# Joint 512-column mLSTM projections, an earlier last key, and a reordered opening in a two-layer mixer kernel on one core

## The chip, the cores and the metric

The kernel runs on one core of one Trainium2 chip. The metric is the device time of that core in microseconds. TensorE (PE) multiplies, VectorE (DVE) and ScalarE (ACT) work on vectors, GpSimd (POOL) does a few helpers, SyncE (SP) issues the DMAs. TensorE takes weights of 128 x 128 and streams 128 to 512 columns past them; its results land in PSUM, which has eight banks of 512 fp32 columns per partition here.

## The reference, cut to what matters

1024 latent tokens and 256 context tokens of width 1024 pass through two layers. Each layer has one input projection, eight bidirectional mLSTM heads and eight neighbourhood attention heads, one output projection and a squared-ReLU MLP.

```python
for l in range(DEPTH):                       # 2
    need_ctx = l < DEPTH - 1
    mod = silu_c @ w_ada[l] + b_ada[l]       # six shifts, scales and gates
    h  = rmsnorm(x,  norm1_g[l]) * (1.0 + sc1)  + sh1
    hc = rmsnorm(xc, norm1_g[l]) * (1.0 + sc1c) + sh1c
    y, yc = token_mixers(h @ w_in[l], hc @ w_in[l], ...)
    x = x + g1 * (y @ w_out[l])
    x = x + g2 * sq_relu_mlp(h2, w_mlp1[l], w_mlp2[l])
# mLSTM, per head, 64-token chunks, both directions:
s   = einsum('bhtd,bhsd->bhts', q, k) * w_intra
num = w_prev * (q @ C) + s @ v;   h = num / max(|qn|, exp(-m))
C   = w_c * C + (w_s * k)^T v
y   = head_layernorm(h_fwd + h_bwd) * sigmoid(o)
```

`w_in` has columns q, k, v, o of the mLSTM, q, k, v of the attention and the gates. The context rows of layer 1 are only read as keys and values, so its queries and gates o are not computed.

## The kernel before, in words

Products are made in fp32 from three passes: each operand is split into a rounded high part and a rest, and `mm3` (L85 to L87) adds high x high, high x rest and rest x high in PSUM. A weight chunk of 128 x 1024 is loaded to `wraw` (2 buffers), cast by ScalarE to `whi` (L79) and subtracted by the vector engine to `wlo` (L80); there are 4 pairs of split buffers. PSUM is cut into two banks of tag "mm" for projections and six of tag "q" for the rest.

Tokens are taken in five tiles of 256 (tile 0 is the context). In the opening (0 to some 57 us) x, the modulation weights and the first weights are loaded, x is squared, scaled and normed, and the first projections run on half of the depth. L1410 and L1411 sum the squares, L1416 scales x, L149 multiplies by the modulation weights, L171 copies their row of sums, L174 turns it, L184 makes the factor A, L1426 and L868 apply it and split x.

Then `mlstm_kv` projects keys, values and gates of the first head pair (288 columns), `gates` makes the decay tables (L329, L349), and `na_values` projects the first half of the attention's values, copied to `wraw` by L619 and stored. The pair's keys are rotated (`rope`, L399 to L403), turned by TensorE (L421, copied by L422), weighted (`vw`, L468), multiplied to chunk states (L470) and linked forwards (L478) and backwards (L459).

`mlstm_out` takes four head pairs by five tiles (four tiles in layer 1). For each it projects q and o of this pair, 256 columns, two token blocks side by side in one "mm" bank. Beside it runs a second generator, `along`: it projects k and v of the next pair, also 256 columns, or for the last pair the second half of the attention's values. Each projection is 48 matmuls of 256 columns. A tile then goes on: exponential of o (L529), rope, transposes of q (L550) and their copy (L552), scores and state product (L561, L562), weights `wt` (L545), P (L571), P·V (L573), normalizing (L576 to L599), transposes of the result (L603) and their store. After the stage the attention starts with its own key and query projections at 512 columns.

The order within each engine is fixed when the program is built; the generators' yields decide which pieces meet, and small steps of the next layer's modulation (`fill`, L149) are strung between.

## Time and profile before

| | |
|---|---|
| median of 3 runs | 2970.12 us (2970.05 to 2971.06) |
| profiled execution | 2972.53 us |
| its span, first to last instruction | 2970.7 us |
| mean granted TensorE clock | 0.995 |
| TensorE, vector engine, ScalarE busy | 98%, 71%, 42% |
| opening | 0 to 57 us |
| first pair, gates, values | 57 to 129.4 and 1640 to 1717.7 us |
| mLSTM stage, layers 0 and 1 | 129.4 to 472.6 and 1717.7 to 2018.5 us |

The other time is neighbourhood attention, output projection and MLP of both layers. Matmul records overlap: a matmul's busy time contains its drain, while the next has begun. So the step from one start to the next tells how fast TensorE gets on, and the idle column what it waited for.

### The profile page before, as it was taken

What the parts mean: (1) busy time and instruction counts of PE and PEld (TensorE: products, weight loads), DVE (VectorE), ACT (ScalarE), POOL (GpSimd) and SP (SyncE); (2) the same over time, 40 slices, a digit from 0 to 9 for tenths busy, and PEclk for the clock granted to TensorE, in tenths of its full rate; (3) what the DMA queues carried; (4) which work ended last, traced back from release to release, by engine and by line L of the source; (5) the groups of instructions that cost most, each with busy time, mean ns of one, the idle gap of its engine ahead of it and who ended that gap; (6) DMA issues with size and microseconds to landing.
All of it is one profiled execution on the core that took longest, in us unless ns stands there. A gap on an engine that the chain in (4) does not pass through costs nothing. (4 is left out here: it accounts for less than half of the span.)

```text
span 2970.7 us, 49781 instructions
## 1 busy us (share of the span) xinstructions
PE 2905.2 (98%) x18900; PEld 2515.7 (85%) x18900; DVE 2105.7 (71%) x4805; ACT 1256.3 (42%) x2350; POOL 71.8 (2%) x117
## 2 busy tenths in 40 slices
PE   7999999999999999999999999999999999999998
PEld 4899998888888888888889989998878788888888
DVE  6666786777686655587676667776775887768765
ACT  5322233555463333344454322234554633334453
POOL 0000000001000000000000000000010000000000
PEclk9999999999999999999999999999999999999999
DMA  6444213235545444696765254213346364469673
GB/s 234 159 129 141 67 53 103 79 118 172 176 140 182 143 143 147 232 329 223 260 205 182 75 163 145 93 39 118 97 144 208 114 197 151 156 224 318 217 238 112
DMA packets 295841, 477.21 MB, mean 161 GB/s; under 512 B 20625, under 2 KB 149649, under 8 KB 295601
## 3 DMA queue, kind: packets, MB, share of 16 engines
q1 hardware_dynamic: 295600, 474.04, 48.2%
q8 instruction: 148, 2.42, 0.3%
q14 instruction: 93, 0.75, 0.1%
HBM read 378.37 MB, written 95.58 MB: 160 GB/s over the span
## 5 line engine op out<-in xcount | busy, mean ns | idle before, releaser
L85 PE MATMUL q<-ah,whi 128*128 128x512 f32 (+1 forms) x1512 | 563.6, 373 | 1.1 <-ACT whi L867 0.7
L86 PE MATMUL q<-al,whi 128*128 128x512 f32 (+1 forms) x1512 | 563.0, 372 | 0.0
L87 PE MATMUL q<-ah,wlo 128*128 128x512 f32 (+1 forms) x1512 | 560.9, 371 | 1.1 <-DVE wlo L868 1.1
L85 PE MATMUL mm<-whi,ah 128*128 128x256 f32 (+1 forms) x1440 | 418.3, 290 | 0.2 <-ACT kva L442 0.2
L86 PE MATMUL mm<-wlo,ah 128*128 128x256 f32 (+1 forms) x1440 | 412.7, 287 | 0.0
L87 PE MATMUL mm<-whi,al 128*128 128x256 f32 (+1 forms) x1440 | 412.2, 286 | 0.0
L85 PE MATMUL mm<-ah,whi 128*128 128x512 f32 (+1 forms) x1080 | 372.7, 345 | 0.6 <-ACT ah L826 0.6
L86 PE MATMUL mm<-al,whi 128*128 128x512 f32 (+1 forms) x1080 | 372.3, 345 | 0.0
L87 PE MATMUL mm<-ah,wlo 128*128 128x512 f32 (+1 forms) x1080 | 371.9, 344 | 0.0
L85 PEld LDWEIGHTS q<-ah,whi 128*128 128x128 f32 x1512 | 284.9, 188 | 54.9 <-issue 4.0
L87 PEld LDWEIGHTS q<-ah,wlo 128*128 128x128 f32 x1512 | 285.0, 188 | 51.9 <-DVE wlo L868 1.9
L86 PEld LDWEIGHTS q<-al,whi 128*128 128x128 f32 x1512 | 285.1, 189 | 50.4 <-issue 2.1
L85 PEld LDWEIGHTS mm<-whi,ah 128*128 128x128 f32 x1440 | 277.1, 192 | 8.7 <-issue 4.0
L86 PEld LDWEIGHTS mm<-wlo,ah 128*128 128x128 f32 x1440 | 277.1, 192 | 1.9 <-issue 1.7
L87 PEld LDWEIGHTS mm<-whi,al 128*128 128x128 f32 x1440 | 277.0, 192 | 0.7 <-issue 0.7
L85 PEld LDWEIGHTS mm<-ah,whi 128*128 128x128 f32 x1080 | 204.6, 189 | 26.5 <-ACT ah L826 1.3
L87 PEld LDWEIGHTS mm<-ah,wlo 128*128 128x128 f32 x1080 | 204.8, 190 | 24.8
L86 PEld LDWEIGHTS mm<-al,whi 128*128 128x128 f32 x1080 | 204.6, 189 | 24.6
L867 ACT CAST ah<-raw 128x512 fp32r<-128x512 f32 (+1 forms) x264 | 145.0, 566 | 118.2 <-PE q L87 59.6
L868 DVE TENSOR_TENSOR al<-raw,ah 128x512 fp32r<-128x512 f32 (+1 forms) x264 | 158.4, 620 | 31.0 <-ACT ah L867 30.9
L80 DVE TENSOR_TENSOR wlo<-wraw,whi 128x1024 fp32r<-128x1024 f32 (+2 forms) x90 | 109.3, 1216 | 97.3 <-ACT whi L79 96.2
L868 DVE TENSOR_TENSOR wlo<-raw,whi 128x1024 fp32r<-128x1024 f32 x84 | 102.7, 1223 | 103.6 <-ACT whi L867 103.3
(285 smaller groups left out, 5209.4 us busy)
## 6 DMA issues: line engine op xcount, KB each, us to landing
raw<-w SPq DMA_DIRECT2D x168, 512.0 KB
raw<-hid SPq DMA_DIRECT2D x104, 512.0 KB
wada<-w_ada SPq DMA_DIRECT2D x96, 512.0 KB
wraw<-w SPq DMA_DIRECT2D x80, 512.0 KB
hid<-hb SPq DMA_DIRECT2D x128, 256.0 KB
hid<-ht SPq DMA_DIRECT2D x96, 256.0 KB
gb<-gscr SPq DMA_DIRECT2D x36, 512.0 KB
wraw<-w_out SPq DMA_DIRECT2D x32, 512.0 KB
```

Of the source, the lines that this page charges most:

```text
L80: nc.vector.tensor_sub(lo[:, :n], raw[:, :n], fview(hi[:, :n]))
L85: mm(out, lh, rh, start=start, stop=False, skip_group_check=True)
L86: mm(out, lh, rl, start=False, stop=False, skip_group_check=True)
L87: mm(out, ll, rh, start=False, stop=stop, skip_group_check=True)
L867: ins = self.nc.scalar.copy(hi, src)
L868: self.nc.vector.tensor_sub(lo, src, fview(hi))
```

## The change

1. The weights are laid out anew: `w_j` has for each pair [k and v of the next pair | q and o of this pair], for the last pair [second half of the values | q and o]. `project_j` multiplies them in one go: per token block 24 matmuls of 512 columns into a whole "mm" bank, two banks per tile. Four split chunks serve a pair instead of two and two.
2. `mlstm_tile` gets the projected columns and yields once more, between scores and P·V. The keys' turn, the states and the back links (`kv_turn`, `kv_state`, `kv_back`) are called by the step instead of by a generator beside it. Rope and the copies of o, k and v work on 128 columns of each bank instead of 256 of one.
3. The first pair's last two keys are turned before the values; the values are staged in `kva` buffers instead of `wraw`.
4. The attention's first two key projections (`qk_project`, 256 and 512 columns) are issued in the mLSTM stage's last step.
5. In the opening the squares of the third group, the scalings, the W splits and the norms are ordered anew, with eight buffers of squares instead of four.

```diff
+    def project_j(self, W, i, hi, lo, cols):
+        for u in range(2):
+            acc = self.bank("mm")
+            for k in range(KT):
+                wh, wl = W[k // 2]
+                ws = slice((k % 2) * 512, (k % 2) * 512 + cols)
+                self.mm3(acc[:, :cols], self.toktile(hi[k], 2 * i + u), ...
...
     def mlstm_kv(self, l, hi, lo, W, accs):
...
+            if i > 1:
+                self.kv_turn(0, i - 2)
+            yield
+        self.kv_turn(0, NT // 2 - 2)
+        self.kv_turn(0, NT // 2 - 1)
+        yield
...
     def mlstm_out(self, l, hi, lo, need_ctx, W):
+            if n and i == 0:
+                W = self.joint_weights(l, pr)
+            mine = need_ctx or i > 0
+            accs = self.project_j(W, i, hi, lo, 512 if mine else 256)
+            if pr < 3:
+                self.kv_take(pr + 1, i, accs)
+            else:
+                self.value_store(l, 1, i, [a[:, 0:256].unsqueeze(1) for a in accs])
+            t = self.mlstm_tile(l, pr, i, [a[:, 256:512].unsqueeze(1) for a in accs]) if mine else iter(())
...
+            if n == len(seq) - 1:
+                Wq.extend(self.qk_weights(l, 0, which) for which in (1, 0))
+                keys.append(self.qk_project(Wq[0], 0, hi, lo))
+                next(t, None)
+                run_all(before)
+                keys.append(self.qk_project(Wq[0], 1, hi, lo))
+                run_all(t)
+                return Wq, keys
+            if i == n2 and pr < 3:
+                self.kv_turn(pr + 1, i)
+                self.kv_state(pr + 1, i)
+                self.kv_back(pr + 1)
+            later = ahead(n + 1)
+            next(t, None)
+            next(later, None)
+            run_all(before)
+            if i < n2 and pr < 3:
+                self.kv_turn(pr + 1, i)
+                self.kv_state(pr + 1, i)
             t, before = later, t
...
     def mlstm_tile(self, l, pr, i, acc):
             S.append(sb)
+        yield
         for u in range(2):
...
     def opening(self, xp, ap0, xsrc, hi, lo):
-        q = [squares(0), squares(1)]
-        r = [self.rstd(*z) for z in q]
-        scale(0, r[0])
-        q = squares(2)
-        scale(1, r[1])
-        scale(2, self.rstd(*q))
-        W = [self.split_raw(t, n) for t, (_, n) in zip(raws, chunks)]
-        steps(first, 2)
+        run_all(squares(0, q[0]))
+        run_all(squares(1, q[1]))
+        r0 = self.rstd(*q[0])
+        rest = squares(2, q[2])
+        steps(rest, 2)
+        r1 = self.rstd(*q[1])
+        scale(0, r0)
...
+        W = [self.split_raw(raws[z], chunks[z][1]) for z in range(2)]
+        r2 = self.rstd(*q[2])
+        scale(1, r1)
+        scale(2, r2, range(6))
```

On TensorE, in the mLSTM stage of layer 0, before: a projection of q and o has ended eleven rows earlier, eight modulation matmuls and the scores of the tile before (L561, L562) follow, and from the last score matmul on stands this (ah, al, whi, wlo are the split parts; L573 P·V, L550 and L603 the transposes of q and of the result):

```order
L562 MATMUL q<-cst,qT 128x130
L573 MATMUL q<-kva,P 128x65 x4
L85 MATMUL mm<-whi,ah_87 128x256
L86 MATMUL mm<-wlo,ah_87 128x256
L87 MATMUL mm<-whi,al_111 128x256
L85 MATMUL mm<-whi,ah_90 128x256
L86 MATMUL mm<-wlo,ah_90 128x256
L87 MATMUL mm<-whi,al_114 128x256
L85 MATMUL mm<-whi,ah_93 128x256
L573 MATMUL q<-kva,P 128x65 x2
L550 MATMUL q<-consts,qr 128x128 x2
L603 MATMUL q<-consts,hs 128x128 x2
```

The same place of a tile after, from the last projection matmul on (L605 and L606 scores, L618 P·V, L594 and L648 transposes, L469 keys' turn, L489 states).

```order
L87 MATMUL mm<-whi,al_133 128x512
L618 MATMUL q<-kva,P 128x65 x8
L149 MATMUL q<-wada,silu 32x256 x8
L85 MATMUL mm<-whi,ah_88 128x512
L86 MATMUL mm<-wlo,ah_88 128x512
L87 MATMUL mm<-whi,al_112 128x512
L85 MATMUL mm<-whi,ah_91 128x512
L594 MATMUL q<-consts,qr 128x128 x2
L648 MATMUL q<-consts,hs 128x128 x2
L469 MATMUL q<-consts,kt 128x128 x2
L489 MATMUL q<-vw,kt 64x130 x4
L605 MATMUL q<-qT,kva 128x128
```

Forty-four wide matmuls of the projection follow behind the scores, then P·V. The transposes of q moved ahead of the scores: P·V, modulation and four wide matmuls stand between them and the end of their projection.

On ScalarE, at the end of the first pair of layer 0, before: L619 copies the values, L79 casts weights, L422 copies the last two turned keys, L473 the states, L546 the weights of the scores.

```order
L619 COPY wraw<-mm 128x512
L79 CAST whi<-wraw 128x1024
L546 ACTIVATE wt<-wt 128x2x256
L79 CAST whi<-wraw 128x1024
L619 COPY wraw<-mm 128x512
L422 COPY kva<-q 128x256 x2
L473 COPY kvb<-q 128x130 x2
```

After, from the last two turned keys (L470) on; L290 and L291 belong to the gates, L668 copies the values.

```order
L470 COPY kva<-q 128x256
L459 COPY kva<-mm 128x2x64
L470 COPY kva<-q 128x256
L79 CAST whi<-wraw 128x1024
L290 ACTIVATE ge<-ge 64x1280
L291 ACTIVATE ge<-ge 64x1280
L668 COPY kva<-mm 128x512
```

The keys' copies moved ahead of the gates and the values, and a cast of a weight chunk now stands ahead of the gates.

On the vector engine in the opening, before: L1410 adds squares, L1416 scales x, L80 splits the weights, L171 copies the row of modulation sums, L178 and L184 make A.

```order
L1410 TENSOR_TENSOR tmp<-tmp 128x512 x4
L1416 TENSOR_TENSOR x_147<-x_147,ssq 128x512 x4
L1416 TENSOR_TENSOR x_148<-x_148,ssq 128x512 x4
L1416 TENSOR_TENSOR x_149<-x_149,ssq 128x512 x4
L1416 TENSOR_TENSOR x_150<-x_150,ssq 128x512 x4
L80 TENSOR_TENSOR wlo<-wraw,whi 128x864 x2
L80 TENSOR_TENSOR wlo<-wraw_175,whi 128x576
L171 COPY arow<-mm 64x512
L178 TENSOR_TENSOR mod<-mm,consts 128x8 x2
```

After, with L1452 for the squares and L1458 for the scaling:

```order
L1452 TENSOR_TENSOR tmp<-tmp 128x512 x2
L80 TENSOR_TENSOR wlo<-wraw,whi 128x864 x2
L1458 TENSOR_TENSOR x_147<-x_147,ssq 128x512 x4
L1458 TENSOR_TENSOR x_148<-x_148,ssq 128x512 x4
L1458 TENSOR_TENSOR x_149<-x_149,ssq 128x512 x4
L1458 TENSOR_TENSOR x_150<-x_150,ssq 128x512 x2
L171 COPY arow<-mm 64x512
L178 TENSOR_TENSOR mod<-mm,consts 128x8 x2
```

Two splits stand ahead of the scaling, two scalings and the third split behind the row of sums.

## Rows read from the trace of the kernel before

**Rows 1.** The page's first part: busy time of each engine, its share of the span, and instructions.

```profile
PE 2905.2 (98%) x18900; PEld 2515.7 (85%) x18900; DVE 2105.7 (71%) x4805; ACT 1256.3 (42%) x2350; POOL 71.8 (2%) x117
```

**Rows 2.** Windows: length, then busy time and instructions of PE, weight loads, DVE, ACT and POOL, granted clock, DMA share, GB/s. The mLSTM stages of both layers, and the loading in the opening.

```profile
129.40:472.60 343.20, 336.89 (x3019) 316.49 (x3018) 252.72 (x961) 100.86 (x244) 18.90 (x35) 1.00 0.33 104
1717.70:2018.50 300.80, 296.62 (x2673) 279.20 (x2670) 215.88 (x812) 85.14 (x206) 15.30 (x31) 0.99 0.33 105
5.00:40.00 35.00, 23.14 (x66) 7.91 (x68) 23.89 (x46) 18.32 (x36) 0.00 (x0) 0.91 1.03 372
```

**Rows 3.** Timeline of TensorE (start, busy time): the first and the last of 17 consecutive matmuls of 256 columns in the mLSTM stage, and the first and the last of 46 consecutive ones of 512 columns in a later stage.

```profile
307.01 0.28 PE L86 MATMUL mm<-wlo,ah 128*128 128x256 f32 x1
...
308.93 0.28 PE L87 MATMUL mm<-whi,al 128*128 128x256 f32 x1
...
2449.78 0.39 PE L85 MATMUL q<-th,whi 128*128 128x512 f32 x1
...
2459.98 0.39 PE L85 MATMUL q<-ah,whi 128*128 128x512 f32 x1
```

**Rows 4.** TensorE's groups by shape in the mLSTM stage of layer 0: count, busy time and mean of one, idle time before.

```profile
L85 PE MATMUL mm<-whi,ah 128*128 128x256 f32 x639 | 185.0, 289 | 0.0
L86 PE MATMUL mm<-wlo,ah 128*128 128x256 f32 x640 | 183.2, 286 | 0.0
```

**Rows 5.** Timeline of TensorE right behind the second row of group 3: the first score matmuls, the return and the matmul after it.

```profile
309.14 0.50 PE L561 MATMUL q<-qT,kva 64*128 64x128 f32 x4
...
310.33 0.38 PE L85 MATMUL mm<-whi,ah 128*128 128x256 f32 x1
310.56 0.28 PE L86 MATMUL mm<-wlo,ah 128*128 128x256 f32 x1
```

**Rows 6.** TensorE's groups over the whole span; after the second bar the idle time before them and what ended it.

```profile
L573 PE MATMUL q<-kva,P 128*128 128x65 f32 x576 | 82.1, 269 | 10.2 <-DVE P L571 9.2
...
L470 PE MATMUL q<-vw,kt 128*64 128x130 f32 x320 | 24.7, 292 | 8.2 <-ACT kva L422 7.9 <-DVE vw L468 0.3
```

**Rows 7.** Timelines at the end of layer 0's first pair: TensorE, ScalarE (idle time and what ended it in brackets), and the DMA queue's issues of weight chunks.

```profile
127.07 1.63 PE L470 MATMUL q<-vw,kt 128*64 128x130 f32 x12 [3.63 <-ACT kva L422]
...
119.22 1.05 ACT L79 CAST whi<-wraw 128x1024 fp32r<-128x1024 f32 x1 [5.46 <-DMA wraw<-w_m]
...
125.21 1.04 ACT L79 CAST whi<-wraw 128x1024 fp32r<-128x1024 f32 x1 [0.79 <-DMA wraw<-w_m]
...
113.60 0.34 SPq L72 DMA_DIRECT2D wraw<-w_m  x1
...
119.96 0.33 SPq L72 DMA_DIRECT2D wraw<-w_m  x1
```

**Rows 8.** Timelines of the vector engine and of TensorE in the opening.

```profile
24.48 9.71 DVE L1416 TENSOR_TENSOR x<-x,ssq 128x512 f32<-128x512 f32 x16
34.11 2.69 DVE L80 TENSOR_TENSOR wlo<-wraw,whi 128x864 fp32r<-128x864 f32 x3
36.72 0.68 DVE L171 COPY arow<-mm 64x512 f32<-64x512 f32 x1
...
38.78 0.41 DVE L1426 TENSOR_SCALAR x<-x,A,mod 128x256 f32<-128x256 f32 x1
...
32.51 1.05 PE L149 MATMUL mm<-wada,silu 128*32 128x512 f32 x4 [0.64 <-DMA wada<-w_ada]
37.54 0.66 PE L174 MATMUL mm<-consts,arow 64*128 64x64 f32 x4 [3.98 <-DVE arow L171]
38.13 5.33 PE L149 MATMUL mm<-wada,silu 128*32 128x512 f32 x12
43.39 0.53 PE L85 MATMUL q<-whi,ah 128*128 128x288 f32 x1
```

**Rows 9.** Timelines: TensorE's modulation matmuls and P·V with the return behind them; the last matmul of a projection and the vector engine's start on its bank; rope products of 128 columns and a value copy of 128 columns in the first pair. The last row is of the waits in the mLSTM stage of layer 0: us in total, times, longest.

```profile
142.72 1.07 PE L149 MATMUL q<-wada,silu 128*32 128x256 f32 x16
...
145.54 1.08 PE L573 MATMUL q<-kva,P 128*128 128x65 f32 x8 [0.55 <-DVE P L571]
146.43 0.36 PE L85 MATMUL mm<-whi,ah 128*128 128x256 f32 x1
...
350.57 0.28 PE L87 MATMUL mm<-whi,al 128*128 128x256 f32 x1
...
350.89 0.42 DVE L399 TENSOR_TENSOR ropea<-mm,cos 128x256 f32<-128x256 f32 x1 [0.26 <-PE mm L87]
...
77.57 0.29 DVE L399 TENSOR_TENSOR ropea<-mm,cos 128x128 f32<-128x128 f32 x1 [2.14 <-ACT gr L429]
77.78 0.28 DVE L399 TENSOR_TENSOR ropeb<-mm,sin 128x128 f32<-128x128 f32 x1
...
78.10 0.27 ACT L442 COPY kva<-mm 128x128 f32<-128x128 f32 x1
...
DVE ropea L399 <- ACT og L529: 37.6, 10, 5.4
```

**Rows 10.** The vector engine's groups in the mLSTM stage of layer 0: the splits of weight chunks.

```profile
L80 DVE TENSOR_TENSOR wlo<-wraw,whi 128x1024 fp32r<-128x1024 f32 x16 | 20.1, 1253 | 6.2 <-ACT whi L79 6.1
```

**Rows 11.** Timelines at the end of layer 0's gates: ScalarE's last step and TensorE's first use.

```profile
110.06 0.20 ACT L329 ACTIVATE wc<-wc 64x10 f32<-64x10 f32 x1
...
111.15 1.12 PE L349 MATMUL q<-wc,sel 64*64 64x10 f32 x32
```

More of the change, by code (lines that the diff above doesn't have):

```diff
@@ new lines, in kv_begin, with kv_take @@
+    def kv_begin(self, pr):
+        self.mst[pr] = dict(kT=[], va=[], kts=[], kvb={})
+    def kv_take(self, pr, i, accs):
+        nc, st = self.nc, self.mst[pr]
+        kt = self.mp.tile([128, 2, 128], F32, name="kt", bufs=6)
+        kva = self.mp.tile([128, 516], F32, name="kva", bufs=MB)
+        acc = [a[:, :256].unsqueeze(1) for a in accs]
+        if i:
+            self.rope([a[:, :, 0:128] for a in acc], i, kt)
+        else:
+            for u, a in enumerate(acc):
+                nc.vector.tensor_copy(kt[:, u:u + 1, :], a[:, :, 0:128])
+        va = kva[:, 0:260].rearrange("p (u h e) -> p u h e", u=2, h=2)
+        for u, a in enumerate(acc):
+            nc.scalar.copy(va[:, u:u + 1, :, 0:64], a[:, :, 128:256].rearrange("p u (h e) -> p u h e", h=2))
+        nc.gpsimd.memset(va[:, :, :, 64:65], 1.0)
+        st["kts"].append(kt)
+        st["va"].append(va)
+        st["kT"].append(kva[:, 260:516].rearrange("p (u t) -> p u t", u=2))
@@ L1365, in mixers @@
                 self.setup_out(l)
-                Wq = []
-                def first(values):
-                    for i, _ in enumerate(values):
-                        if i == NT // 2 - 2:
-                            Wq.extend(self.qk_weights(l, 0, which) for which in (1, 0))
-                        yield
-                self.mlstm_out(l, hi, lo, need_ctx, W, lambda pr: twice(self.mlstm_kv(l, pr + 1, hi, lo)) if pr < 3 else first(self.na_values(l, 1, hi, lo)))
+                Wq, keys = self.mlstm_out(l, hi, lo, need_ctx, W)
         with self.open(name=f"na{l}") as self.np_:
@@ L1411, in squares, with scale, norm @@
                 nc.tensor.matmul(p[:, :n], self.ones[:], sq[0][:, :n], start=f == 0, stop=f == KT - 2)
[L1412 to L1415 removed]
+                yield
+        def scale(gi, r, fs=range(KT)):
+            for f in fs:
                 nc.vector.tensor_mul(xf(x, gi, f), xf(x, gi, f), r[:, :GROUPS[gi][1]])
[L1418 removed]
+        def norm(todo):
             sh = self.mod[:, 0:8, :]
@@ L1446, in opening @@
+        r0 = self.rstd(*q[0])
[3 more added lines that the diff above has]
+        scale(0, r0)
+        steps(first, 1)
+        steps(rest, 1)
+        steps(first, 1)
+        steps(rest, 1)
+        W = [self.split_raw(raws[z], chunks[z][1]) for z in range(2)]
+        r2 = self.rstd(*q[2])
+        scale(1, r1)
+        scale(2, r2, range(6))
+        for z in range(6):
             steps(first, 1)
             steps(second, 1)
+            if z == 3:
+                nc.sync.dma_start(raws[2][:], d["w_kvg"][0][:, 1728:])
@@ L1448, in opening @@
         steps(first, 1)
-        norm(range(4))
-        halves, accs = (range(4), range(4, 8)), {}
+        norm([(gi, f) for gi in range(2) for f in A])
+        scale(2, r2, range(6, 8))
         steps(second, 3)
-        accs[0] = self.project_g(W, 0, hi, lo, "q", ks=halves[0])
-        steps(second, 3)
-        accs[1] = self.project_g(W, 1, hi, lo, "q", ks=halves[0])
+        accs[0] = self.project_g(W, 0, hi, lo, "q", ks=A, us=(0,))
+        steps(second, 1)
+        self.project_g(W, 0, hi, lo, "q", accs[0], A, (1,))
@@ L1455, in opening @@
         steps(second, 2)
-        accs[2] = self.project_g(W, 2, hi, lo, "q", ks=halves[0], us=(0,))
+        accs[1] = self.project_g(W, 1, hi, lo, "q", ks=A, us=(0,))
         steps(second, 1)
-        self.project_g(W, 2, hi, lo, "q", accs[2], halves[0], (1,))
-        norm(range(4, 8))
+        self.project_g(W, 1, hi, lo, "q", accs[1], A, (1,))
+        steps(second, 1)
+        accs[2] = self.project_g(W, 2, hi, lo, "q", ks=A, us=(0,))
+        steps(second, 1)
+        norm([(0, f) for f in B])
@@ L1460, in opening @@
+        W.append(self.split_raw(raws[2], chunks[2][1]))
+        norm([(1, f) for f in B])
+        norm([(2, f) for f in (*A, *B)])
+        self.project_g(W, 2, hi, lo, "q", accs[2], A, (1,))
         for i in range(3):
-            self.project_g(W, i, hi, lo, "q", accs[i], halves[1])
-        return W, accs, self.value_weights(0, 0, range(1))
+            self.project_g(W, i, hi, lo, "q", accs[i], B)
+        return W, accs, self.value_weights(0, range(1))
     def run(self):
@@ L1609, in run_all @@
         pass
-def twice(g):
-    for _ in g:
-        next(g, None)
-        yield
 def chain(*gs):
```

255 lines of the change are left out of this document (116 added, 139 removed).

## The prediction

> **What bounds the kernel now.** I read the page's busy times first: TensorE works in 98% of the span [rows 1], so time can go only where its stream becomes denser or where it stands still. The windows by stage then show which stages the change can reach [rows 2]: the two mLSTM stages last 343.2 and 300.8 us, TensorE is busy in 336.9 and 296.6 of them at full clock, the vector engine in 252.7 and 215.9, the DMA engines in a third. They are bound by how fast TensorE gets through its list. The opening is the opposite: between 5 and 40 us the DMA share is 1.03, TensorE waits. Third I read the step from one matmul's start to the next, since the busy time of one (0.28 or 0.39 us) overlaps its neighbours [rows 3], and last what TensorE waited for [rows 6 to 8].
>
> **Columns.** From 307.01 to 308.93 sixteen 256-column matmuls pass, 0.120 us each; from 2449.78 to 2459.98 forty-five 512-column ones, 0.2267 us each [rows 3]. One wide matmul for two narrow ones saves 0.240 - 0.227 = 0.0133 us. By the code, layer 0 has 1920 narrow matmuls in this stage (keys and values of three pairs 720, queries and gates of four 960, neighbourhood values 240), and [rows 4] show 639 + 640 + 640 of them; they become 960 wide ones. Layer 1 has 1728; its context tiles need only the left half, so 192 narrow ones stay and 1536 become 768. That is 960 + 768 = 1728 pairs, 23.0 us. Bounds: nothing, if a wide matmul took twice 0.120, and 23.
> The Trainium skill ("TensorE: Matmul & The Clock Gate", section "Back-to-back issue gap") gives a warm gap of N/2.4 + 2.5 ns, a fixed cost of only 2.5 ns per matmul. By it the columns would bring 1728 x 2.5 ns = 4.3 us. The trace has 120 and 227 ns where the formula has 109 and 216, so here the fixed part is 13 ns and I keep 23 us.
>
> **Interruptions.** Between two projection matmuls the step is 0.12; from the last one to the first score matmul it is 0.21 (308.93 to 309.14), and the first pair after the return is 0.23 apart (310.33 to 310.56) [rows 3, 5]. So one excursion costs about 0.2 beyond its own work. Counted in the instruction orders, the two mLSTM stages have 88 and 73 excursions before, 57 and 54 after: 50 fewer. At 0.16 (some of the small work is moved behind other small work, where the entry is not saved) 8 us; bounds 0 and 10.
>
> **Waits for P.** TensorE stood 10.2 us in all before the P·V matmuls (L573), 9.2 of it for the vector engine's P [rows 6], because P·V came straight behind its scores. Now forty-four wide matmuls, 10 us, stand between (first order excerpts). I take 9; bounds 0 and 10.
>
> **First pair.** L470 stood 8.2 us, 7.9 for ScalarE's kva copy [rows 6]: 3.63 at 127.07 and the rest in layer 1. ScalarE was held by the cast of a weight chunk which was issued at 119.96 and could be cast at 125.21 [rows 7]; behind it in its queue stood the copies of the last two keys. They are now ahead of the values, and the values no longer share the raw weight buffers. What is late next there is the fourth chunk of the joint weights, of which the first projection has need only 18 wide matmuls (4 us) in. I take 7; bounds 3 and 8.
>
> **Opening.** The row of modulation sums (L171) waited on the vector engine behind sixteen scalings, 24.48 to 34.19, and three W splits, while TensorE had ended the first modulation product at 33.6; its next work came at 37.54 after 3.98 us, A was ready only at 38.8 and the first projection at 43.39 [rows 8]. In the new order two splits and fourteen scalings stand before the row; squares of the third group overlap the first's scaling, and the third split and the third group's norm go behind. The loading itself, full until about 40 us, is not shortened: the row can come no sooner than the last of that weight (32.5 + 1.05). I take the row at 34 and the first projection 5 us sooner; twelve modulation products, 5.3 us at 38.13, must still pass, now between projections. Bounds: 0, where the loading decides, and 8, all of the gap and the norm.
>
> **What is added: queries wait.** Before, the scores, most of P·V and seven narrow matmuls stood between the end of the q projection and the transposes of q (L550). Now there are only eight P·V matmuls (0.89 from 145.54 to 146.43), in 22 of the 36 steps eight modulation matmuls (half of 1.07), and four wide ones: from the start of the last projection matmul 0.3 + 0.9 + 0.5 + 1.0 = 2.7 us, or 2.2 without modulation [rows 9]. Against that stands a chain on one bank: the vector engine starts 0.32 after the start of a 256-column matmul (350.57 to 350.89), so 0.43 after a wide one. Two key rope products (step 0.21, the last 0.28) end at 0.92. ScalarE's value copy and exponential, 0.27 each and partly overlapped, end at 1.4. The vector engine has meanwhile an hh sum (as long as a rope product of 256 columns, 0.42) and two halves of the key; the two q products end about 2.2, another hh and the two q halves about 3.0. So the transposes wait 0.25 us with modulation and 0.75 without: 22 x 0.25 + 10 x 0.75 = 13 (four of the other tiles are context tiles without rope). I take 12; bounds 0 and, with 1 us more on the vector engine, 45.
> The order on a bank is visible before: DVE ropea waited 37.6 us for ScalarE's og [rows 9]. The Trainium skill ("PSUM — Partial Sum Buffer", section "PSUM bank collisions raise a hardware error") says why four readers of one bank cannot run two abreast: any two engines on one bank and quadrant have to be ordered. If they could, the 0.45 of ScalarE would leave the chain, and by the same working some 3 us would be lost instead of 12.
>
> **What is added: pair changes.** Four splits instead of two now fall into one step, with nine back links of the state. Four chunks of cast and split are 4 x 1.25 = 5 us of the vector engine [rows 10]. Chunks three and four need the raw buffers of one and two, and a load took 5.6 and 5.3 us from issue to cast [rows 7], so ScalarE's cast of chunk three stands ahead of its qT copy and comes about a microsecond late. Six changes at 1.2: 7 us; bounds 0 and 6 x 5.3 = 32.
>
> **Gate chain.** wc left ScalarE at 110.26 and TensorE took it at 111.15 [rows 11]; a joint weight cast now stands ahead in ScalarE's queue. The slack hides 0.9; I add 1 us for both layers, bounds 0 and 3. The moved keys of the attention are the same matmuls, at 512 and 256 columns, before the stage's end instead of behind it, and give cover there; nothing. Narrower rope and copies add some 9 us to a vector engine with 90 us free in layer 0; only where they stand in the chain above do they count.
>
> **Sum.** -23 - 8 - 9 - 7 - 5 + 12 + 7 + 1 = -32 us. The profiled execution took 2972.53 (span 2970.7 and 1.8 around it), so 2940.5 for the like; the median of the runs is 2.4 lower, 2970.12, which gives 2938.
>
> **Rivals.**
> *The query wait is covered.* If the vector engine runs ahead as the 90 us free suggest, 12 goes: 2926. Against it: the chain is latency, not load.
> *The columns do not pay.* If a wide matmul in this stream, with a weight load ahead of each, took 0.2375 us and not 0.2267, a pair would save 2.5 ns, and the sum loses 18.7: 2957. Against it stand two sets of rows at full clock [rows 3], the wide ones with a weight load ahead of each too. (It is also what the formula above gives.)
> *The weights come late at each pair change.* Each change then waits for a whole load, 32 instead of 7: 2963. For it: two raw buffers for four chunks; against it: the DMA share is only a third there.
> *Slower: the evacuation of the two banks decides.* With both banks filled by one tile, the q transposes and the scores behind them wait on the vector engine in every tile. The gains are 52, the other costs 8; from 44/36 = 1.2 us per tile the change loses. That is 0.8 more than I reckon, as much as two further 0.42 us operations ahead of the rope on the vector engine; at 1.4 it ends at 2976. For it: that engine is busy in 74% of the stage, and works its list in order; against it: in the new order the P products stand well before the last rope.
> The opening bringing nothing, bound by loading, gives 2943, inside the forecast's own range.
>
> **Chances.** Forecast 0.50 (own range 2926 to 2950), covered wait 0.22, columns 0.06, late weights 0.13, slower 0.09. Less than 0.2% (6 us) cannot be told from no change: faster 0.87, no change 0.05 (the worst third of late weights), slower 0.08. Range 2916 to 2963: the low end lets the covered wait come with 10 us more from opening and interruptions, the high end is the late weights.
>
> **What would show it.** In the new profile the wide matmuls of the stage should start 0.227 apart; DVE P should vanish among the waits of P·V; the wait of 3.6 and 4.3 before the state matmuls should be gone; new idle time should stand before the transposes of q, for DVE qr, about 12 us in all, and 1 us at each pair change; the first projection should start near 38. I am wrong if the wide step is 0.24, if the idle before qr exceeds 40 us, or if the mLSTM stages together shorten by less than 15 us.

## The result and the profile after

The changed kernel takes 2945.64 us (median of four runs, 2943.84 to 2946.74), the kernel before on the same chip 2970.59 (four runs, 2970.05 to 2971.75). The ratio is 0.9915, with a 95% interval of 0.9898 to 0.9932: faster by 25 us. The forecast was 2938 with a range of 2916 to 2963, a gain of 32. One of the five executions of run 7 below took 5148.85 us at a granted clock of 0.75 and is left out of all comparisons.

The span of the profiled executions went from 2970.7 to 2944.4, 26.3 us. Cut at six events on TensorE that both kernels have (in each layer the first gate matmul L283, the last matmul of the gate tables L359 and the first attention score), it splits as follows (us):

| stretch | before | after | measured | forecast |
|---|---|---|---|---|
| opening: start to layer 0's first gate matmul | 70.1 | 68.6 | -1.5 | -5 |
| layer 0's gates: from there to the end of its gate tables | 44.2 | 48.4 | +4.2 | +0.5 |
| from there to layer 0's first attention score | 384.1 | 366.5 | -17.6 | -14 |
| layer 1's gates | 38.4 | 42.1 | +3.7 | +0.5 |
| layer 1, end of gate tables to first attention score | 341.9 | 326.3 | -15.6 | -14 |
| all the rest | 2092.1 | 2092.5 | +0.5 | 0 |

The gain is wholly in the two mLSTM stages, and it is larger there than forecast (33.2 against 28). The opening gained 1.5 instead of 5, and the gates of the two layers lost 7.9 instead of 1.

The page's first line, which answers to [rows 1]:

```profile
PE 2883.7 (98%) x17172; PEld 2423.0 (82%) x17172; DVE 2118.5 (72%) x4927; ACT 1264.9 (43%) x2426; POOL 68.0 (2%) x117
```

TensorE has 18,900 - 17,172 = 1728 instructions fewer, which is the number of pairs in the prediction, and stays busy in 98% of a shorter span. The kernel is still bound by TensorE's list.

The windows (length, busy time and instructions of PE, weight loads, DVE, ACT, POOL, then granted clock, DMA share, GB/s) of the mLSTM stages, here from the end of the gate tables to the first score, and of the loading [rows 2]:

```profile
117.00:483.50 366.50, 359.69 (x2298) 293.69 (x2297) 277.17 (x1067) 117.75 (x310) 16.73 (x35) 1.00 0.36 114
1690.80:2017.10 326.30, 321.56 (x2129) 264.30 (x2128) 240.88 (x911) 102.31 (x265) 13.56 (x31) 1.00 0.36 119
5.00:40.00 35.00, 29.13 (x92) 10.89 (x93) 25.70 (x51) 21.50 (x43) 0.00 (x0) 0.95 1.04 384
```

The loading moves its data at the same rate as before (DMA share 1.04), and TensorE is busy for 29.1 instead of 23.1 us in it: work was drawn into the loading. That it gained so little time all the same is the subject of a point below.

TensorE's groups over the whole span (after the bar busy time and mean; after the second bar the idle time before them and what ended it) answer to [rows 6]:

```profile
L618 PE MATMUL q<-kva,P 128*128 128x65 f32 x576 | 69.8, 273 | 0.0
L489 PE MATMUL q<-vw,kt 128*64 128x130 f32 x320 | 25.6, 284 | 3.0 <-DVE vw L487 2.7 <-DVE cst L496 0.3
L594 PE MATMUL q<-consts,qr 128*128 128x128 f32 x72 | 14.5, 276 | 0.6 <-DVE qr L416 0.6
L605 PE MATMUL q<-qT,kva 64*128 64x128 f32 x288 | 35.7, 309 | 1.4 <-ACT qT L596 1.3
L648 PE MATMUL q<-consts,hs 128*128 128x128 f32 x72 | 13.8, 274 | 5.2 <-DVE hs L644 5.2
L283 PE MATMUL mm<-consts,gr 128*128 128x128 f32 x20 | 4.1, 290 | 2.8 <-ACT gr L429 2.7
L85 PE MATMUL mm<-whi,ah 128*128 128x512 f32 (+2 forms) x864 | 314.8, 365 | 4.2 <-ACT kva L459 3.7 <-DVE st L285 0.5
```

The rows of before that answer to the transposes, the gates and the narrow projection, with next to no wait:

```profile
L550 PE MATMUL q<-consts,qr 128*128 128x128 f32 x72 | 14.3, 275 | 0.0
L603 PE MATMUL q<-consts,hs 128*128 128x128 f32 x72 | 14.1, 273 | 0.3 <-DVE hs L599 0.3
L283 PE MATMUL mm<-consts,gr 128*128 128x128 f32 x20 | 3.9, 283 | 0.0
L85 PE MATMUL mm<-whi,ah 128*128 128x256 f32 (+1 forms) x1440 | 418.3, 290 | 0.2 <-ACT kva L442 0.2
```

The wait for P (10.2 before L573) is gone, that for ScalarE's kva copy (7.9 before L470) is gone too and has left 2.7 for vw. The new wait that I feared most, for the queries (L594), is 0.6. Three waits that I did not forecast stand there instead: 5.2 before the transposes of hs (L648), at the end of each layer's stage, 2.7 before the gates (L283), and 3.7 for ScalarE's copy of the first pair's values (kva, L459) before a projection in the gates.

TensorE's timeline shows where they stand:

```profile
68.63 0.55 PE L283 MATMUL mm<-consts,gr 128*128 128x128 f32 x3 [2.36 <-ACT gr L429]
...
88.02 0.39 PE L85 MATMUL mm<-whi,ah 128*128 128x256 f32 x1 [1.55 <-ACT kva L459]
...
127.74 0.44 PE L489 MATMUL q<-vw,kt 128*64 128x130 f32 x4 [1.80 <-DVE vw L487]
...
352.84 0.40 PE L87 MATMUL mm<-whi,al 128*128 128x512 f32 x1
353.07 1.90 PE L618 MATMUL q<-kva,P 128*128 128x65 f32 x16
354.90 1.07 PE L149 MATMUL q<-wada,silu 128*32 128x256 f32 x16
...
356.93 0.38 PE L594 MATMUL q<-consts,qr 128*128 128x128 f32 x2
...
463.39 0.41 PE L648 MATMUL q<-consts,hs 128*128 128x128 f32 x2 [2.50 <-DVE hs L644]
463.55 0.48 PE L85 MATMUL q<-ah,whi 128*128 128x512 f32 x1
```

### The profile page after: what moved, and what is told of

Read it like the earlier page. It is cut to its first block, busy times and chain, and to the rows that moved or that the text cites. A ratio compares the mean times of both kernels' runs of the same rounds, so it can differ in the third digit from the quotient of the medians.

```text
span 2944.4 us, 46505 instructions
## 1 busy us (share of the span) xinstructions
PE 2883.7 (98%) x17172; PEld 2423.0 (82%) x17172; DVE 2118.5 (72%) x4927; ACT 1264.9 (43%) x2426; POOL 68.0 (2%) x117
## 4 chain that ended last, share of the span: by engine, by line
PE 67%; DVE 4%; DMA 2%; ACT 1%; issue 1%; SPq 1%; POOL 0%; DVEq 0%; ACTq 0%; POOLq 0%
PE q L85 13%; PE q L86 13%; PE q L87 13%; PE mm L85 8%; PE mm L86 8%; PE mm L87 8%; PE q L866 1%; PE q L618 1%; DMA raw<-hid 1%; PE q L840 0%; DMA wraw<-yscr 0%; PE q L825 0%; PE q L149 0%; DMA wraw<-w 0%; SPq L1385 0%
## 5 line engine op out<-in xcount | busy, mean ns | idle before, releaser
L85 PE MATMUL mm<-ah,whi 128*128 128x512 f32 (+1 forms) x1112 | 384.7, 346 | 3.4 <-ACT ah L876 1.8
L86 PE MATMUL mm<-al,whi 128*128 128x512 f32 (+1 forms) x1112 | 384.1, 345 | 0.0
L87 PE MATMUL mm<-ah,wlo 128*128 128x512 f32 (+1 forms) x1112 | 383.8, 345 | 0.0
L85 PE MATMUL mm<-whi,ah 128*128 128x512 f32 (+2 forms) x864 | 314.8, 365 | 4.2 <-ACT kva L459 3.7
L86 PE MATMUL mm<-wlo,ah 128*128 128x512 f32 (+2 forms) x864 | 311.2, 360 | 0.0
L87 PE MATMUL mm<-whi,al 128*128 128x512 f32 (+2 forms) x864 | 310.3, 359 | 0.0
L85 PEld LDWEIGHTS mm<-whi,ah 128*128 128x128 f32 x864 | 164.3, 190 | 35.6 <-issue 7.3
L87 PEld LDWEIGHTS mm<-whi,al 128*128 128x128 f32 x864 | 164.4, 190 | 23.8 <-issue 0.7
L86 PEld LDWEIGHTS mm<-wlo,ah 128*128 128x128 f32 x864 | 164.6, 190 | 22.4 <-issue 0.2
L85 PE MATMUL q<-th,whi 128*128 128x512 f32 x384 | 150.0, 391 | 2.1 <-DVE s L1082 2.0
```

The costliest lines, as they stand in the source:

```text
L85: mm(out, lh, rh, start=start, stop=False, skip_group_check=True)
L86: mm(out, lh, rl, start=False, stop=False, skip_group_check=True)
L87: mm(out, ll, rh, start=False, stop=stop, skip_group_check=True)
```

## The experiments

All ratios are to the kernel before, timed on the same chip; differences to the changed kernel are between medians (2945.64). The runs come from three chips, on which the median of the kernel before was 2971.50 (runs 1, 2, 4, 6), 2972.13 (runs 5, 7, 8, 10) and 2971.59 (runs 3, 9, 11), and the changed kernel came out 1.0 higher when it was timed again (run 11). So a difference of 2 or 3 us between two medians is at the edge of the scatter.

**1. Columns alone undone.** Each wide matmul becomes two of 256 columns on the two halves of the same bank; order and tiles stay. The accumulation then alternates between the halves of a bank, and the kernel's sums come out different (why was not looked into), so only the time is read.

```
-  self.mm3(acc[:, :cols], ..., wh[:, ws], wl[:, ws], k == 0, k == KT - 1)
+  for c in range(0, cols, 256):
+      ws = slice((k % 2) * 512 + c, (k % 2) * 512 + c + 256)
+      self.mm3(acc[:, c:c + 256], ..., wh[:, ws], wl[:, ws], k == 0, k == KT - 1)
```

> Every joint projection matmul of 512 columns is made as two of 256 over the same weights; all else is as in the changed kernel. Theory (a narrow pair takes 0.240 us, a wide matmul 0.227): 1728 pairs give back 23 us, 2945.6 becomes about 2968, and the narrow step in the new trace is 0.120. Rival 1 (the fixed cost is 2.5 ns per matmul): 4 us, 2950. Rival 2 (the gain came from the waits alone, the columns were hidden): no change, 2946.

Measured: 2969.75 us (2967.66 to 2975.5), ratio 0.9998 (0.9989 to 1.0007), 24.1 more than the changed kernel. TensorE's timeline has two narrow ones in a row 0.12 apart, as in [rows 3]:

```profile
331.54 0.28 PE L87 MATMUL mm<-whi,al 128*128 128x256 f32 x1
331.66 0.28 PE L85 MATMUL mm<-whi,ah 128*128 128x256 f32 x1
```

This confirms the 23 us of the columns against the rivals of 4 and 0. With narrow matmuls, all the rest of the change together gains 1 us against before, which is no more than the scatter.

**2. Scores and P·V in one step again.** Columns stay wide; the `yield` that parts the two goes, so P·V follows its own scores.

```
             S.append(sb)
-        yield
         for u in range(2):
```

> The new yield between scores and P·V is taken out, so that P and P·V are issued right behind the scores as before. Theory (the projection between them hides the vector engine's P): TensorE's wait for P, 10.2 us before and none now, comes back, 8 to 10 us, 2954. Rival (with wide projections the P·V is moved by the order anyway and finds its P ready): below 2 us, 2946.

Measured: 2964.51 us, ratio 0.9974 (0.9963 to 0.9986), 18.9 more (single runs from 2955.63 to 2969.93): twice what the theory gives for the returning wait. Its groups on TensorE (here L617 is P·V):

```profile
L617 PE MATMUL q<-kva,P 128*128 128x65 f32 x576 | 78.8, 272 | 6.7 <-DVE cst L496 3.9 <-DVE P L615 1.2 <-DVE hh L620 0.5
L594 PE MATMUL q<-consts,qr 128*128 128x128 f32 x72 | 15.8, 292 | 3.3 <-DVE qr L416 3.1
```

P·V waits 6.7 and the queries 3.3, together 10; but only 1.2 of the 6.7 is put down to P itself, most to cst, the vector engine's states. From the end of the gate tables to the first attention score the two layers are 8.5 and 12.3 us longer than in the changed kernel. Idle time makes 9 of these 21. TensorE also leaves the projection stream 78 and 64 times instead of 50 and 47 and spends 7 us more between its matmuls (idle time and a wide step of 0.227 per departure taken off). So the parting is worth more than its wait. That these 7 come from the number of departures is likely, but no run shows it by itself.

**3. The kernel before with the parting alone.** The opposite test: narrow columns, all else as before, but scores and P·V in two steps.

```
             if i == NT // 2 - 1:
                 run_all(beside)
+            next(t)
             t, before = later, t
...
             S.append(sb)
+        yield
```

> The kernel before with one part of the change alone: scores and P·V are parted by a yield, P·V going behind the next pair's key projection; 256-column projections, opening, first pair and keys as before. Theory (the wait for P is what the parting removes, 10.2 us in the profile of before): 8 to 10 us faster, 2962. Rival 1 (as in the run without the yield, the parting is worth 19 us, excursions included): 2952. Rival 2 (the two projections of before already gave the order room, so that parting only moves the waits): no change, 2971.

Measured: 2976.63 us, ratio 1.0016 (1.0007 to 1.0025): 5 us slower than before. Its groups (L575 is P·V, L551 the transposes of q):

```profile
L575 PE MATMUL q<-kva,P 128*128 128x65 f32 x576 | 70.0, 275 | 0.0
L551 PE MATMUL q<-consts,qr 128*128 128x128 f32 x72 | 14.8, 287 | 14.5 <-DVE qr L403 13.8 <-DVE qr L535 0.6
```

The wait for P is gone entirely, and 14.5 us of wait for the queries have taken its place: the wait moved. Excursions (departures of TensorE from the projection stream) fell here too, from 88 to 58 in layer 0, and saved nothing that shows. The parting needs the rest of the change: in the order of before it costs 5 us, and all the rest without it gains 7 (run 2 against before on the same chip), all together 25. It is not the narrow columns that make the wait for the queries: run 1 has them too, with the parting in the joint order, and waits only 0.8:

```profile
L595 PE MATMUL q<-consts,qr 128*128 128x128 f32 x72 | 14.5, 275 | 0.8 <-DVE qr L417 0.8
```

**4. The old opening.** Order, fewer temporaries and the early load of the third weight chunk as before.

```
-        self.wide, self.ntmp = 0, 8
+        self.wide, self.ntmp = 0, 4
...
-        run_all(squares(0, q[0]))
-        run_all(squares(1, q[1]))
...
+        q = [squares(0), squares(1)]
+        r = [self.rstd(*z) for z in q]
```

> The opening is put back to the old one, four buffers of squares included; all else as changed. Theory A (the first projection starts 6.8 us sooner, but the third group's norm, now wholly behind the second modulation product, gives it back before the gates): the time stays within 2 us of 2945.6, the first projection starts at 43.4 and the gate matmuls' first use of the tables (113.8 now) is within 2 us of that. Theory B (the reordered opening is worth 5 us, as predicted): 2951.

Measured: 2944.86 us, ratio 0.991 (0.9893 to 0.9927), 0.8 less than the changed kernel. Its first projection starts at 41.6 instead of 36.6, and its gate tables end at 114.4 instead of 117.0. The five microseconds won at the first projection are lost again before the tables end.

**5. The third group's norm back into the pause.** Of the new opening only the first half of the third group's norm is moved, from the end of the chain to behind its scaling.

```
         scale(2, r2, range(6, 8))
+        norm([(2, f) for f in A])
         steps(second, 3)
...
-        norm([(2, f) for f in (*A, *B)])
+        norm([(2, f) for f in B])
```

> In the changed opening, the first half of the third token group is normed directly behind the other two groups' first halves, while the vector engine waits for the second modulation product (idle from 42.7 to 48.7), not at the end. Theory (the gain of the earlier first projection was given back because that norm, some 3.7 us, stood at the end of the chain): TensorE's waits at 55 to 69 (3.7 us in all) mostly vanish, first use of the gate tables 113.8 becomes about 110, the time 2942. Rival (the second product's row or the splits are delayed instead): no change, 2946.

Measured: 2941.49 us, ratio 0.9899 (0.9883 to 0.9914), 4.1 less. The vector engine's timeline, first of the changed kernel, then of this run:

```profile
48.66 0.68 DVE L171 COPY arow<-mm 64x512 f32<-64x512 f32 x1 [5.96 <-PE mm L149]
...
66.81 1.46 DVE L918 TENSOR_TENSOR al<-x,ah 128x512 fp32r<-128x512 f32 x2
```

```profile
45.89 1.47 DVE L918 TENSOR_TENSOR al<-x,ah 128x512 fp32r<-128x512 f32 x2
...
49.07 0.68 DVE L171 COPY arow<-mm 64x512 f32<-64x512 f32 x1 [1.72 <-PE mm L149]
```

The changed kernel's vector engine stands still for 5.96 us before the second row of modulation sums, and does the third group's norm behind it, until 68; the gates wait 2.36 us there, and 1.33 in two waits at 55. With the norm in the pause the wait before the gates is gone (that of 0.94 at 55 stays), and the tables end at 113.3. Of these 3.7 us, 2.1 come before the first gate matmul; the other 1.6 are the size of one stretch at the lower clock (1.7), which the profile of the changed kernel has behind that wait (window from 70 to 75 us under run 11).

**6. The first pair's last key turned later again.** The two copies and turns go behind the step's end.

```
+        yield
         self.kv_turn(0, NT // 2 - 2)
         self.kv_turn(0, NT // 2 - 1)
-        yield
```

> The first pair's last two keys are turned behind the values again; the values stay in their new buffers and the weights are joint. Theory (the wait came from the order: the copies stood behind a weight cast in ScalarE's queue): 3 to 4 us per layer return before the state matmuls, for ACT kva, 2951. Rival (the wait came from the values sharing the raw weight buffers, which delayed the load): no change, 2946.

Measured: 2948.43 us, ratio 0.9927 (0.9913 to 0.9942), 2.8 more; the scatter of single runs (2946.45 to 2952.24) is as large. The wait before the states is longer again, but put down to the vector engine. The vector engine's timeline and TensorE's:

```profile
126.33 0.88 DVE L589 SCALAR_TENSOR_TENSOR wt<-gb,tab,mask 128x128 f32<-128x128 f32 x3 [5.36 <-ACT kva L470]
```

```profile
131.20 0.70 PE L489 MATMUL q<-vw,kt 128*64 128x130 f32 x4 [3.36 <-DVE vw L487]
```

TensorE's wait before the states rises from 3.0 to 4.8 us in all, where 3 to 4 per layer were expected, and none of it is put down to ScalarE's copies. By the profile they stand one step further back: the vector engine, whose vw comes last, had stood idle for 5.36 us until the copies ended (4.70 in the changed kernel, up to ScalarE's cast ahead of them). With the keys turned late again, most of the 8.2 us of before stay away, so the early turn has some 1.8 of the 5.2 us won there. Which other part of the change has the rest (values out of the raw weight buffers, joint weights) was not tested.

**7. Joint weights held behind the last rope and copy.** Their split on the vector engine stands ahead of the rope of the last key in the changed kernel.

```
-            W = self.joint_weights(l, 0)
+            with self.tc.issue_after(roped.ins), self.tc.issue_after(taken.ins):
+                W = self.joint_weights(l, 0)
```

> The first pair's joint weight chunks are split only behind the rope and the value copies of the last key tile on the vector engine and ScalarE; TensorE's order is unchanged. Theory (in the changed kernel two splits of 1.2 us stand ahead of that rope, so the value copy, the bank and TensorE's first value projection come 1.55 us late in each layer): the waits at 88.0 and 1660.3 for ACT kva shrink below 0.5, 2 to 3 us in all, some 2943; the low clock that followed the stall in layer 1 may go with it, 1.7 us more. Rival (the bank is late because of the gate work, or the splits are then late for the first joint projection): no change, 2946.

Measured: 2946.88 us (2944.65 to 2951.88), ratio 0.992 (0.9906 to 0.9933): no change. In its timeline of TensorE the first wait shrinks from 1.55 to 0.51, and the next, for vw, grows from 1.80 to 2.31:

```profile
87.31 0.39 PE L85 MATMUL mm<-whi,ah 128*128 128x256 f32 x1 [0.51 <-ACT kva L459]
...
127.56 0.44 PE L489 MATMUL q<-vw,kt 128*64 128x130 f32 x4 [2.31 <-DVE vw L487]
```

In layer 1 the same pair goes from 1.54 to 0.50 and from 0.38 to 1.64. The time moved to the next wait on the same engine.

**8. A third attention key in the last step.** The projection of the third group's keys is put into the stage's last step, ahead of the transposes of hs.

```
                 keys.append(self.qk_project(Wq[0], 1, hi, lo))
+                keys.append(self.qk_project(Wq[0], 2, hi, lo, tag="q"))
                 run_all(t)
```

> The attention's third key projection (24 matmuls of 512 columns, 5.4 us) is issued in the mLSTM stage's last step too, into a bank of the other tag. Theory (the transposes of the last result wait 2.5 and 2.7 us for the vector engine because the second key projection is too short a cover): both waits vanish, 5 us, 2941. Rival (the vector engine's chain is longer than that cover as well, or the time is waited for later, at the queries): less than 2 us, 2944 to 2946.

Measured: 2938.04 us (2935.91 to 2942.06), ratio 0.9889 (0.9876 to 0.9903), 7.6 less. The transposes at the end no longer wait:

```profile
464.95 0.40 PE L87 MATMUL q<-ah,wlo 128*128 128x512 f32 x1
465.19 0.38 PE L649 MATMUL q<-consts,hs 128*128 128x128 f32 x2
```

This removes the 5.2 us of L648; the other 2.4 are of the size of the scatter.

**9. No attention keys in the last steps.** Both calls are taken out, and the keys are projected where the attention wants them.

```
-                keys.append(self.qk_project(Wq[0], 0, hi, lo))
...
-                keys.append(self.qk_project(Wq[0], 1, hi, lo))
```

> The changed kernel without the attention's two early key projections; the last step then has nothing beside the last tile's P·V and normalizing, and the attention projects all keys itself. Theory (the keys are the only cover there): TensorE waits for the last tile's P and its transposes some 8 us longer in each layer's end, of which the earlier start of nothing else is regained: 2955 to 2962. Rival (the attention's own projections are drawn forward by the order, whoever issues them): within 3 us of 2945.6.

Measured: 2942.72 us (2941.73 to 2945.38), ratio 0.9903 (0.9888 to 0.9918), no loss. The waits before the transposes of hs (L646 here) are about the same (2.50 and 2.48): in layer 0, 48 matmuls of the attention's projections stand in the last steps ahead of that wait in either kernel, so the order draws them forward in any case. This part of the change is worth nothing by itself; what run 8 adds is one projection more ahead of the wait.

**10. Runs 5, 7 and 8 together.** No new edit.

> The three edits together. If each removes its own wait and nothing new ends later, their gains add: 2.5 + 5 + 3.7, about 2934.5. If they share a bound (the end of the gate chain for the first and the third), about 2938.

Measured: 2934.67 us (2933.4 to 2939.53), ratio 0.9879 (0.9866 to 0.9893): 11.0 less than the changed kernel (the three alone add to 10.5) and 36 less than before. This is the first of the two expectations: the gains add. Its idle time on TensorE is 39.0 us, against 52.7 in the changed kernel and 57.5 before.

**11. The changed kernel again, unaltered.**

> The changed kernel itself once more, on the same chip as the two above, as their measure: 2944 to 2948. For the granted clock: if a stall of TensorE of more than 1.4 us is followed by a stretch at the lower clock only in some executions, this profile shows other such stretches than the first one at the same stalls (the first has 55, 70 and 1660 us, and none behind the stalls of 1.8 at 127.7, 2.5 at 463.4 and 2.7 at 2000); if the kernel decides it, it shows the same.

Measured: 2946.66 us (2944.46 to 2948.45), ratio 0.9913 (0.9897 to 0.993). Windows of TensorE's granted clock (last but two) behind the three stalls, in the first profile of the changed kernel and in this one:

```profile
70.00:75.00 5.00, 5.00 (x30) 4.98 (x29) 4.14 (x16) 1.86 (x9) 0.22 (x2) 0.69 0.33 105
90.00:95.00 5.00, 5.00 (x52) 4.44 (x50) 3.38 (x4) 3.77 (x4) 0.21 (x1) 1.00 0.41 139
130.00:135.00 5.00, 5.00 (x23) 4.12 (x23) 4.77 (x22) 1.21 (x3) 0.00 (x0) 1.00 0.44 163
```

```profile
70.00:75.00 5.00, 4.06 (x32) 4.04 (x32) 4.86 (x14) 2.50 (x12) 0.22 (x2) 1.00 0.33 103
90.00:95.00 5.00, 5.00 (x32) 5.00 (x31) 3.46 (x3) 3.86 (x4) 0.00 (x0) 0.68 0.44 147
130.00:135.00 5.00, 4.58 (x17) 2.92 (x18) 4.86 (x20) 1.27 (x6) 0.00 (x0) 0.66 0.94 326
```

The stalls ahead of these windows are alike (2.36 and 2.35; 1.55 and 1.55; 1.80 and 1.82 us), and the dips are not: the first execution dips behind the first, the second behind the other two.

## Why the prediction was right, and where it was off

**Columns, -23: right.** The step of the wide matmul is 0.227 in the changed kernel (25 steps from 347.17 to 352.84 are 5.67 us), and run 1 gives 24.1. The rival of columns that do not pay falls. The gap of N/2.4 + 2.5 ns, by which I reckoned 4.3 us, stands in the Trainium skill ("TensorE: Matmul & The Clock Gate", section "Back-to-back issue gap") for an isolated matmul; for a stream of weight loads and matmuls the section itself says that the formula is off, which I had not taken in. In this stream the fixed part is the 13 ns of [rows 3].

**Waits for P, -9: right.** 10.2 us went to 0.0. But run 2 shows that putting P·V back costs 19, with only 1.2 of wait for P, and run 3 that in the order of before the wait goes as well, and turns up before the queries. The term was right as a row of the idle list, and no price of the edit that takes it out.

**Queries wait, +12: wrong, it is 0.6.** The step that failed is the cover of 2.7 us, from "only eight P·V matmuls (0.89)" and "eight modulation matmuls (half of 1.07)". I took rows of the instruction order as matmuls, and each of these fp32 rows is two in the trace; [rows 9] show half of a tile's P·V. The timeline above has sixteen P·V (from 353.07) and sixteen modulation matmuls (from 354.90), and the transposes start at 356.93, 4.09 us after the start of the last projection matmul, not 2.7. The chain was also longer than my 3.0, as the vector engine's timeline of the changed kernel shows (key's rope, q's rope, second half of q):

```profile
353.27 0.29 DVE L412 TENSOR_TENSOR ropea<-mm,cos 128x128 f32<-128x128 f32 x1 [3.25 <-PE mm L87]
...
354.86 0.28 DVE L412 TENSOR_TENSOR ropea<-mm,cos 128x128 f32<-128x128 f32 x1
...
356.13 0.28 DVE L416 TENSOR_TENSOR qr<-ropea,ropeb 128x128 f32<-128x128 f32 x1
```

It ends at 356.41, 3.57 after the same start, 0.5 ahead of TensorE. Tiles without modulation are covered too: seven to nine wide matmuls stand there, not the four of the excerpt (seven at 406.26, 420.83 and 435.42), and the queries are ready 0.6 us ahead of TensorE. So the rival of the covered wait is what happened, for a reason that I had not given: the cover was half as long again, while the chain came out as latency, as I held. That the mechanism is real shows in run 3, where it costs 14.5.

**Interruptions, -8: not in the sum.** Excursions fell even more than counted, from 88 and 73 to 50 and 47 (from the end of the gate tables to the first attention score of each layer). But the time between the stream's matmuls (start to start, without idle time and the last matmul's own step) fell only from 102.2 to 100.9 us in layer 0 and from 87.3 to 85.7 in layer 1, and the lower clock of the next point is part of these 2.9. My 0.2 came from an excursion to the scores [rows 5], whose matmuls use 64 rows. Excursions to P·V, which uses all 128, cost nothing in the trace of before (0.121 and 0.083 into and out of it, against a step of 0.120), and they are what the parting moved together: 84 of the excursions went to P·V before, 26 after. Run 3 agrees: 51 excursions fewer, no gain.

**First pair, -7: right in place, too small.** The waits before the states fell from 8.2 (7.9 for kva) to 3.0 (2.7 for vw), 5.2 us. More came from the granted clock behind the old stalls, which I had not looked at. In the windows of the trace of before:

```profile
125.00:130.00 5.00, 2.93 (x18) 1.86 (x19) 3.07 (x9) 3.41 (x10) 0.00 (x0) 0.56 0.94 321
130.00:135.00 5.00, 5.00 (x34) 5.00 (x35) 4.53 (x20) 0.93 (x3) 0.00 (x0) 0.76 0.93 297
...
1715.00:1720.00 5.00, 4.41 (x26) 3.30 (x27) 4.16 (x17) 2.01 (x8) 0.00 (x0) 0.62 1.04 358
1720.00:1725.00 5.00, 5.00 (x33) 5.00 (x33) 4.17 (x14) 1.68 (x2) 0.00 (x0) 0.70 0.90 303
```

The 4.27 us stall of layer 1 ended at 1715.33. A clock of 0.62 and then 0.70 over two windows is 3.8 + 3.0 us at 1.2 GHz, half of it lost: 3.4 us; in layer 0, less the part inside the stall, some 2.7. In the profile of after these dips are absent, 6 us in this pair of profiles; in that of run 3, with the same first pair and stalls of 3.47 and 3.21, they last half as long (0.77 and 0.89 in the two windows from 1715). The working "what is late next is the fourth weight chunk" failed: vw was next. The order of the keys is only part of the cause: with the early turn alone undone (run 6), 4.8 of wait stand there and not 8.2.

**Pair changes, +7: too large.** One wait is left, 1.34 us at 377.08, and it is the one described: ScalarE's cast of a chunk (375.70, after 3.04 us of waiting for its load) stands ahead of the copy of qT. It came at one of six changes. No wait of TensorE for a weight chunk itself shows at a pair change; the rival of late weights falls.

**Opening, -5: too large, it is -1.5.** The first projection did start earlier, at 36.6 instead of 43.4 (foreseen 38). The step that failed is "twelve modulation products must still pass, now between projections": I followed the chain to the first projection and not to the last one that needs the norm. The third group's norm stands behind the second row of modulation sums, behind a pause of 5.96 us, and TensorE waits. Of the 6.8 us, 3.7 go into waits (0.94 and 0.39 at 55, 2.36 at 68.63) and 1.7 into a stretch at the lower clock (0.66 in the window from 55 to 60). Runs 4 and 5 show both halves: the whole new opening is worth nothing, and with one call moved it is 3.4 us better than the old one (2941.49 against 2944.86; the tables end 1.1 earlier).

**Gate chain, +1: too small, it is +7.9.** The cast that I counted is on ScalarE; the split of the same chunks on the vector engine costs more. The vector engine's and ScalarE's timelines:

```profile
84.85 2.42 DVE L80 TENSOR_TENSOR wlo<-wraw,whi 128x1024 fp32r<-128x1024 f32 x2 [1.57 <-ACT whi L79]
87.19 0.28 DVE L412 TENSOR_TENSOR ropea<-mm,cos 128x128 f32<-128x128 f32 x1
```

```profile
87.70 0.27 ACT L459 COPY kva<-mm 128x128 f32<-128x128 f32 x1 [1.34 <-DVE ropeb L412]
```

Two splits hold the rope until 87.19, the rope holds the copy, and TensorE waits 1.55 us in both layers. With smaller waits it stands still for 2.3 us in the gates of layer 0 and 2.4 in those of layer 1 (0.0 and 0.2 before). The rest is about what the clock takes: the gates of each layer have one stretch at the lower clock in the profile of after and none before, with 0.69 in the window from 70 to 75 (shown under run 11) and 0.66 in this one of layer 1:

```profile
1660.00:1665.00 5.00, 4.71 (x26) 4.71 (x27) 3.92 (x6) 3.02 (x5) 0.10 (x1) 0.66 0.49 184
```

That is 1.6 to 1.7 us each. Run 7 shows that moving the splits alone only moves the wait.

**End of the stage, 0: +4.9.** "The moved keys give cover there; nothing" is not what came: parting adds a step to each tile, so the last tile's scores, P·V and output now stand with less beside them. The wait before the transposes of hs was 0.3 before; it is 2.8 with the parting alone (run 3), 2.6 with all but the parting (run 2) and 5.2 with both, so the parting has half of it. What the other half comes from was not tested. Run 8 shows that the wait is one for cover, by giving it back; run 9 shows that the moved keys give no more than the order draws forward without them.

**The slower rival** (evacuation decides) needed 1.2 us per tile and got 0.6 in all.

So the sign and the range were right, and the largest term held. Added up from the traces, start to start on TensorE, the -33 us of the two mLSTM stages are -25 in the projection stream, -3 between its matmuls, -7 of idle time and +2 in the attention's early projections, which are now interrupted by the last tiles. Of the -25, 23 are the columns; the other 2 and the 3 together are no more than the 6 that the clock took behind the old stalls, so nothing is left for fewer excursions. The sum of 32 came near 26 because errors offset each other, which is luck: losses overrated by 17 (queries and pair changes), a first pair underrated by 4 and P by 1 stood against 8 for interruptions, 3.5 for the opening, 7 for the gates, 5 for the end of the stage and 2 for the attention's projections; some 2 us stay unassigned.

## What to carry to other kernels

An idle row tells where a wait stands now, not what an edit that removes it will bring: parting scores and P·V removed the same wait twice, but lost 5 us in the order of before and was worth 19 in the joint one. When a critical chain is sped up in an opening, follow it to its last consumer, and look for work that has slid behind a pause; and when a row of an instruction order is used for time, look in the trace how many instructions it becomes. Here, going into or out of the stream took longer than its step of 0.120 only where matmuls of 64 rows, or with 64 or 32 columns of weights, came between (0.20 to 0.31 in the trace of before, against 0.03 to 0.12 for P·V and the transposes of 128 x 128); that the size is the reason was not tested. So count excursions by kind.

## What was not expected of the hardware

The granted clock behind a stall is not settled by the stall's length in this range. Runs of the same instructions with the same stalls of 1.55, 1.8 and 2.35 us dipped at different ones (run 11), and in the ten microseconds from 125 run 7 has some 6.5 us at the lower clock behind a stall of 2.31 (windows at 0.85 and 0.50), run 3 some 3.4 behind one of 3.47 (0.71 and 0.95). A window at 0.66 to 0.69 is some 3.2 us at 1.2 instead of 2.4 GHz, which costs 1.6 to 1.7 us, as much as the shorter of these stalls. In the trace of before the stalls of 3.63 and 4.27 us were both followed by a dip that reaches over two of these 5 us windows. So a stall of 1.5 to 2 us may cost about twice its length, and single profiles differ by that much.
